# First head of a woven decoder layer: another order of its projection chunks

## The chip, the cores and the metric

The kernel runs on one core of one Trainium2 chip. The metric is the device time of one execution in microseconds (us). Engines are named as the profile names them: PE (TensorE matmuls), PEld (its weight loads), DVE (VectorE), ACT (ScalarE), POOL (GpSimd), SP (the queue that issues DMAs). A "column" below is one column that a matmul streams through the array; at the full granted clock of 2.4 GHz 2,400 columns take a microsecond.

## The reference, cut to what matters

A hybrid decoder layer on 2,064 tokens (16 meta tokens and 2,048 real ones) of width 1,024. One input projection feeds eight heads of stick-breaking attention and, beside them, a gated linear recurrence (RG-LRU); both are normalised, gated with a SiLU and go through one output projection.

```python
u = rmsnorm(h, pre_g)
q, k, v, g_att, x_lru, g_lru = jnp.split(u @ w_in, ...)       # six groups of 1,024 columns
att = rmsnorm(stick_breaking_attention(q, k, v), att_out_g) * jax.nn.silu(g_att)
lru = rmsnorm(rglru_branch(x_lru, ...), lru_out_g) * jax.nn.silu(g_lru)
y = jnp.concatenate([att, lru], axis=-1) @ w_out
return h + rmsnorm(y, post_g)
# attention, per query row: z = q.k * scale; w = exp(log_beta + suffix sum of log(1 - beta)); o = w @ v
# recurrence, per channel: conv of width 4, two gates (sigmoid of 64x64 blocks), h_t = a_t h_(t-1) + b_t
```

## The kernel before

**Tiling.** The projection, the scores and the attention outputs are made in two fp16 pieces, three matmuls for one product. A weight tile of 128 columns of `w_in` is loaded by `load_w`: DMA, a maximum over it (L144), a small matmul that spreads the maximum (L150), then the two pieces (L158 on ACT, L159 on DVE). There are buffers for three weights; a new one is loaded when the last chunk of an old one is done, in a fixed list: k, q, v, LRU gate, attention gate, LRU input of each head. A *chunk* is one weight against up to 512 tokens (8 x 3 matmuls at L174), into one of three PSUM tiles `mm`.

**Attention.** Each of the 16 query tiles of a head has one to three segments of keys. A segment is a chain over all engines: scores on PE (L301, into one of two PSUM tiles `z`), sigmoid on ACT (L305, frees `z`), a mask on POOL (L310), a product scan on DVE (L315), a cast on ACT (L325, L327), a subtraction on DVE (L332, L333), a DMA transpose (L338, `wT<-w`), and the output on PE (L352, `o<-wT,v`). After four query tiles ACT empties `o` (L385, L388).

**The recurrence.** Half a head's LRU input (three `xl` chunks, emptied at L458) makes one half of `Mix`: convolution on DVE (L474, L477), six gate steps (L485, L486, L496, L497, L498, L499), and then for both halves tanh, two exps, a square root on ACT (L507, L510, L514, L523, with ACT table loads wherever the function changes), products on DVE and POOL (L519, L527), a scan on DVE (L531), a square on ACT (L535) and a sum on POOL (L544). The first half of head 0's LRU is done before the attention starts, the second beside it.

**Order.** PE, ACT and DVE run in the order in which a planner emits the work (`weave`, a simulated clock with buffers as `Ring`s). At each step it takes, in this order: something urgent (gate steps, weight loads), the next attention output whose transposed weights are due, the next segment's scores if a `z` tile and a row buffer are free and its pace allows, and otherwise the next matmuls of the chunk that heads the list `fill`. `begin(h)` puts the chunks of head `h` on that list, `K` (k), `Q` (q), `VV` (v), `GL` (LRU gate), `GA` (attention gate) of head `h`, and `XL` (LRU input) of head `h+1`. Only the head of the list is looked at: if it may not start, no later chunk is taken. What holds a chunk back: its weight is not loaded; `GL` needs `"hs" in hd`, the finished recurrence of its head; `K` of a head needs all scores of the head before. `conv(c, m)`, the start of a half of the next head's `Mix`, needs the last `GL` chunk of the head before (`"used" in head[c - 1]`) and its three `XL` chunks.

Head 0's q, k and v are projected before the weave, so its list has only `GA`, `GL` and head 1's `XL`. The last head (7) is written out without the planner; behind it stands the output projection (L1380).

Of the kernel before, what the change touches and what calls it, by code (L numbers as in the profile page):

```python
# [70 lines left out]
def hybrid_layer(nc, tc, I, out):  # L71
# [107 lines left out]
    def unscale(w, f):  # L179
        t = sm.tile([P, 1], F32, name="us", bufs=6)  # L180
        dve.tensor_scalar(out=t, in0=w[2], scalar1=f, scalar2=None, op0=ALU.mult)
        return t
# [91 lines left out]
    def z_scale(wq, wk):  # L274

        t = sm.tile([P, 1], F32, name="zs", bufs=2)
        dve.tensor_scalar(out=t, in0=wq[2], scalar1=wk[2], scalar2=-SCALE / PSC ** 2, op0=ALU.mult, op1=ALU.mult)
        return t
# [538 lines left out]
    def k_then(h, j):  # L817
        def f(ps, t):
            if j == 0:
                kqv["kH"] = kp.tile([P, T], F16, name="kH")  # L820
                kqv["kL"] = kp.tile([P, T], F16, name="kL")
            c0, n = KV_CH[j]
            ev_pair(ps, t, n, kqv["kH"][:, c0:c0 + n], kqv["kL"][:, c0:c0 + n])
        return f
# [3 lines left out]
    def q_then(h, j):  # L828
        def f(ps, t):
            if j == 0:  # L830
                kqv["qH"] = kp.tile([P, S], F16, name="qH")
                kqv["qL"] = kp.tile([P, S], F16, name="qL")
            c0, n = Q_CH[j]
            ev_pair(ps, t, n, kqv["qH"][:, c0 - NM:c0 - NM + n], kqv["qL"][:, c0 - NM:c0 - NM + n])
            head[h]["q"] = t + 1.5 if j == NJ - 1 else None
        return f
# [105 lines left out]
    def ga_then(h, g):  # L942
        def f(ps, t):
            ev_silu(ps, t, head[h]["uga"], rsa, "sa", gate)

        def gate(gt, t):
            if (h, g) not in ots:
                waiting[h, g] = lambda t: gate(gt, t)
                return
            ot = ots.pop((h, g))  # L950
            dve.scalar_tensor_tensor(out=gt, in0=ot, scalar=prm(ATG, h), in1=gt, op0=ALU.mult, op1=ALU.mult)
            t = V(t, 512)
            rot.put(t)

            def store():
                sp.dma_start(out=aa_d[g][h], in_=gt)
                rsa.put(LD(t) - 2)
            plan.at(t, store)
        return f
# [219 lines left out]
    def begin(h):  # L1179

        c = h + 1
        hd = head.setdefault(h, {})
        hd.setdefault("v", [])
        head[c] = {"xs": [], "gates": 0, "v": []}
        hd["zdone"] = hd["odone"] = False

        def scale(to, hh, w):
            def f():
                head[hh][to] = unscale(loaded[w], 1.0)
            return f  # L1190

        def kq():
            hd["wk"] = loaded[f"k{h}"]

        def qs():
            hd["zs"] = z_scale(loaded[f"q{h}"], hd["wk"])

        def vs():
            hd["wv"] = loaded[f"v{h}"]
            hd["vsc"] = unscale(hd["wv"], 1.0 / (VSC * WS))  # L1200
        zs_done = lambda: h == 0 or head[h - 1]["zdone"]
        os_done = lambda: h == 0 or head[h - 1]["odone"]
        K = [Chunk(f"k{h}", *KV_CH[j], k_then(h, j), zs_done, kq if j == 0 else None, j == NJ - 1) for j in range(NJ)]
        Q = [Chunk(f"q{h}", *Q_CH[j], q_then(h, j), None, qs if j == 0 else None, j == NJ - 1) for j in range(NJ)]
        if h == H - 1:
            return K + Q
        VV = [Chunk(f"v{h}", *KV_CH[j], v_then(h, j), os_done, vs if j == 0 else None, j == NJ - 1) for j in range(NJ)]
        GA = [Chunk(f"ga{h}", NM + 512 * g, 512, ga_then(h, g), None, scale("uga", h, f"ga{h}") if g == 0 else None, g == 3)
              for g in range(4)]
        GL = [Chunk(f"gl{h}", NM + 512 * g, 512, gl_then(h, g), lambda: "hs" in hd,  # L1210
                    scale("ugl", h, f"gl{h}") if g == 0 else None, g == 3) for g in range(4)]
        XL = [Chunk(f"xl{c}", (m // 3) * HT + X_CH[m % 3][0], X_CH[m % 3][1], xl_then(c, m), None,
                    scale("uxl", c, f"xl{c}") if m == 0 else None, m == 5) for m in range(6)]
        if h == 0:
            return XL[:2] + GA[:1] + XL[2:4] + GA[1:2] + XL[4:] + GL[:2] + GA[2:] + GL[2:]
        return K + Q + VV + GL[:2] + GA[:1] + GL[2:] + GA[1:2] + XL[:3] + GA[2:] + XL[3:]

    def weave():
        fill, segs = [], []
        for h in range(H - 1):  # L1220
# [5 lines left out]
            segs += hs_  # L1226
        cost = [3.1 * x.L / 1000 + 1.2 for x in segs]
        fill += begin(0)
        nz = no = 0
        begun, due, pace = 0, 0.0, 0.0  # L1230
        while True:
# [37 lines left out]
            if not fill and begun < H - 1:  # L1269
                begun += 1  # L1270
                fill += begin(begun)
# [196 lines left out]
```

## Time and profile before

| | |
|---|---|
| median of 3 runs | 1951.55 us (1946.86 to 1952.28) |
| the profiled execution | 1950.06 us, its span 1948.3 us, mean granted clock 0.975 |
| PE busy | 1817.2 us, 93% of the span |
| DVE, ACT, POOL busy | 1280.1, 1038.4, 395.9 us |
| norms, k, q, v of head 0, first half of LRU 0 | 0 to 164 us |
| woven heads 0 to 6, with q and k of head 7 | 164 to 1443 us |
| head 7 and the output projection | 1443 to 1948 us |

A row of a timeline gives the start, the length and in brackets how long the engine was idle before it and what ended that. A row of stretches gives, for each engine, its busy time; then the granted clock as a share of 2.4 GHz. PE is busy for nearly all of the span, so what can be won is its idle time and the time that it ran at a lower clock.

### The profile page before, as it was taken

How to read it: one execution, taken by the hardware profiler on the slowest of the kernel's cores; microseconds unless marked ns; L12 is line 12 of the kernel's file. 1: busy time of each engine (PE TensorE's matmuls, PEld its weight loads, DVE VectorE, ACT ScalarE, POOL GpSimd, SP SyncE). 2: the span in 40 equal slices, each digit the busy share in tenths (PEclk: the TensorE clock that was granted, in tenths of full speed). 3: DMA queues.
4: the chain of work that ended last, by engine and by line, in shares of the span. 5: the costliest groups of instructions: out<-in, count | busy, mean ns of one | idle time of the engine just before them, and what ended most of it. 6: DMA issues, size and time to landing. Idle time of an engine off the chain costs nothing.

```text
span 1948.3 us, 30797 instructions
## 1 busy us (share of the span) xinstructions
PE 1817.2 (93%) x12048; PEld 1170.5 (60%) x12048; DVE 1280.1 (66%) x1761; ACT 1038.4 (53%) x1764; POOL 395.9 (20%) x460
## 2 busy tenths in 40 slices
PE   3879899699999899999998999999989899999998
PEld 2435565356546655665565566546645578888776
DVE  8546875787578857875895887579865761124554
ACT  6556745755556575556575555655665552132331
POOL 4421100510141132003120401041132010002222
PEclk9989999899999899999999999999999999999999
DMA  5922460364135616441553365146504693245554
GB/s 167 196 52 61 99 130 28 65 127 97 38 79 109 118 29 124 110 82 36 114 115 66 70 136 101 37 80 121 109 19 91 163 225 104 92 160 180 173 173 140
DMA packets 435809, 205.29 MB, mean 105 GB/s; under 512 B 370368, under 2 KB 404160, under 8 KB 435664
## 3 DMA queue, kind: packets, MB, share of 16 engines
q1 hardware_dynamic: 435664, 203.33, 44.3%
q8 instruction: 94, 1.54, 0.3%
q14 instruction: 51, 0.42, 0.1%
HBM read 78.23 MB, written 34.08 MB: 58 GB/s over the span
## 4 chain that ended last, share of the span: by engine, by line
PE 67%; DVE 5%; ACT 3%; DMA 3%; issue 1%; SPq 0%; POOL 0%; DVEq 0%; POOLq 0%; ACTq 0%
PE mm L174 34%; PE y L1380 18%; PE o L352 7%; PE z L301 6%; DMA wT<-w 2%; DVE row L315 1%; DVE lrow L531 1%; DVE w L333 1%; PE mm L496 1%; PE mm L497 0%; ACT lrow L499 0%; ACT row L498 0%; ACT ot L385 0%; DVE wm L144 0%; SPq L338 0%
## 5 line engine op out<-in xcount | busy, mean ns | idle before, releaser
L174 PE MATMUL mm<-uH,wH 128*128 128x512 f16 (+3 forms) x1808 | 624.6, 349 | 12.4 <-DVE qL L219 5.2
L174 PE MATMUL mm<-uL,wH 128*128 128x512 f16 (+3 forms) x1808 | 623.7, 348 | 1.5 <-DMA uL<-w 0.8
L174 PE MATMUL mm<-uH,wL 128*128 128x512 f16 (+3 forms) x1808 | 622.4, 348 | 2.7 <-DVE wL L159 2.7
L174 PEld LDWEIGHTS <-wH 128*128 128x128 f16 x3616 | 341.1, 99 | 310.0 <-issue 39.9
L315 DVE TENSOR_TENSOR_SCAN row<-row 128x656 f32<-128x656 f32 (+6 forms) x208 | 347.6, 1675 | 56.4 <-POOL row L310 47.2
L174 PEld LDWEIGHTS <-wL 128*128 128x128 f16 x1808 | 179.5, 99 | 164.3 <-issue 7.4
L352 PE MATMUL o<-wT,v 128*128 128x128 f16 x3392 | 229.5, 223 | 31.4 <-DMA wT<-w 30.9
L352 PEld LDWEIGHTS <-v 128*128 128x128 f16 x3392 | 211.4, 100 | 69.7 <-issue 35.7
L305 ACT ACTIVATE row<-z,zs 128x656 f32<-128x656 f32 (+6 forms) x208 | 170.7, 825 | 144.1 <-PE z L301 131.4
L333 DVE TENSOR_TENSOR w<-row,w 128x640 f16<-128x640 f32 (+5 forms) x208 | 175.7, 847 | 6.3 <-ACT w L327 5.9
L327 ACT CAST w<-row 128x640 f16<-128x640 f32 (+5 forms) x208 | 155.0, 747 | 41.9 <-DVE row L315 29.1
L301 PE MATMUL z<-kH,qH 128*128 128x328 f16 (+10 forms) x384 | 125.4, 327 | 18.7 <-ACT row L305 18.7
L1380 PE MATMUL y<-woH,aL 128*128 128x512 f32 x352 | 138.8, 394 | 1.2 <-DVE aL L1372 1.2
L1380 PE MATMUL y<-woH,aH 128*128 128x512 f32 x352 | 139.1, 395 | 0.0
L1380 PE MATMUL y<-woL,aH 128*128 128x512 f32 x352 | 138.5, 393 | 0.0
L301 PE MATMUL z<-kL,qH 128*128 128x328 f16 (+10 forms) x384 | 125.2, 326 | 0.0
L301 PE MATMUL z<-kH,qL 128*128 128x328 f16 (+10 forms) x384 | 125.0, 326 | 0.0
L310 POOL TENSOR_SCALAR_AFFINE_SELECT row<-row 128x128 f32<-128x128 f32 x128 | 67.0, 525 | 260.7 <-ACT row L305 243.6
L323 POOL MEMSET w<- 128x80 f16 x128 | 21.7, 169 | 469.1 <-DMA wT<-w 302.0
L486 DVE TENSOR_TENSOR cs<-lrow,cs 64x344 fp32r<-64x344 f32 x96 | 51.6, 538 | 95.9 <-ACT cs L485 88.6
L301 PEld LDWEIGHTS <-qH 128*128 128x128 f16 x768 | 73.2, 99 | 67.6 <-issue 22.3
L1372 DVE TENSOR_TENSOR aL<-araw,aH 128x1024 fp32r<-128x1024 f32 x32 | 39.2, 1224 | 110.4 <-ACT aH L1371 109.1
(225 smaller groups left out, 2544.4 us busy)
## 6 DMA issues: line engine op xcount, KB each, us to landing
wraw<-in_w_in SPq DMA_DIRECT2D x46, 512.0 KB, 3.8
row<-in_x SPq DMA_DIRECT2D x31, 512.0 KB, 4.4
aa_d<-sa SPq DMA_DIRECT2D x32, 256.0 KB, 2.0
al_d<-sl SPq DMA_DIRECT2D x32, 256.0 KB, 2.1
araw<-in_w_out SPq DMA_DIRECT2D x16, 512.0 KB, 4.5
araw<-al_d SPq DMA_DIRECT2D x16, 512.0 KB, 4.1
yl_d<-ys SPq DMA_DIRECT2D x32, 256.0 KB, 2.1
row<-yl_d SPq DMA_DIRECT2D x16, 512.0 KB, 3.2
```

The costliest lines, as they stand in the source:

```text
L174: pe.matmul(out=ps[:, :n], lhsT=a[:, kt, :], rhs=b[:, kt, c0:c0 + n], start=(k == 0), stop=(k == 3 * KT - 1))
L301: pe.matmul(out=z[:, a, :n], lhsT=l[:, qs], rhs=r[:, c], start=(x == 0), stop=(x == 2))
L305: act.activation(out=self.om[:, :L].rearrange("p (a c) -> p a c", a=self.parts), in_=self.z[:, :self.parts, :self.n], func=AF.Sigmoid, sca ...
L310: pool.affine_select(out=d, in_=d, pattern=[[-1, P]], compare_op=ALU.is_gt, fill=1.0, base=0, channel_multiplier=1)
L315: dve.tensor_tensor_scan(out=om, data0=om, data1=om, initial=self.pred.om[:, 0:1] if self.si else WS, op0=ALU.mult, op1=ALU.bypass)
L323: pool.memset(w[:, 3 * NM:P], 0.0)
L327: act.copy(out=w[:, r0:r0 + nb * P], in_=om[:, self.m0:self.L])
L333: dve.tensor_tensor(out=w[:, r0 + nb * P:r0 + 2 * nb * P], in0=om[:, self.m0:self.L], in1=w[:, r0:r0 + nb * P], op=ALU.subtract)
L352: pe.matmul(out=o[:, c], lhsT=l, rhs=r, start=(self.si == 0 and x == 0), stop=(self.last and x == len(prods) - 1))
L486: dve.tensor_tensor(out=cs[oth, :n], in0=xc[own, a:a + n], in1=cs[own, :n], op=ALU.subtract)
L1372: dve.tensor_tensor(out=aL, in0=raw, in1=aH, op=ALU.subtract)
L1380: pe.matmul(out=ps, lhsT=a[:, c, :], rhs=b[:, cs], start=(k == 0), stop=(k == 3 * KT - 1))
```

## The change

One expression in `begin`: the list of head 0's fill chunks.

```diff
         if h == 0:
-            return XL[:2] + GA[:1] + XL[2:4] + GA[1:2] + XL[4:] + GL[:2] + GA[2:] + GL[2:]
+            return GA[:2] + XL[:3] + GL + XL[3:] + GA[2:]
         return K + Q + VV + GL[:2] + GA[:1] + GL[2:] + GA[1:2] + XL[:3] + GA[2:] + XL[3:]
```

The chunks are the same; no instruction is added or taken away. Before, all six `xl` chunks of head 1 came ahead of the four `gl` chunks of head 0. Now the second half of the `xl` chunks stands behind `gl`, and the first two `ga` chunks lead. Because the planner goes on from the state that it is in, the order changes in all later woven heads too.

ACT in head 0, from the second exp of its recurrence (L514) on; `row<-z` are sigmoids of scores, by segment length:

```order
L514 ACTIVATE row<-row,nsp_m_76 128x1032
L305 ACT_TABLE_LOAD
L305 ACTIVATE row<-z,zs 128x640
L325 CAST w<-row 128x2x16
L327 CAST w<-row 128x512
L305 ACTIVATE row<-z,zs 128x656
L523 ACT_TABLE_LOAD
```

```order
L514 ACTIVATE row<-row,nsp_m_76 128x1032
L305 ACT_TABLE_LOAD
L305 ACTIVATE row<-z,zs 128x640
L325 CAST w<-row 128x2x16
L327 CAST w<-row 128x512
L305 ACTIVATE row<-z,zs 128x528
L523 ACT_TABLE_LOAD
```

The 640 in the first piece belongs to query tile 9 (segments of 640 and 656), in the second to tile 8 (640 and 528): the recurrence now stands one query tile earlier.

PE in head 1, at the scores of its query tiles 5 (2 x 392 columns) and 6 (2 x 456):

```order
L301 LDWEIGHTS qL
L301 MATMUL z<-kH,qL 128x392
L301 LDWEIGHTS qH
L301 MATMUL z<-kH,qH 128x456
L301 LDWEIGHTS qH
L301 MATMUL z<-kL,qH 128x456
```

```order
L301 LDWEIGHTS qL
L301 MATMUL z<-kH,qL 128x392
L174 LDWEIGHTS wH
L174 MATMUL mm<-uH,wH 128x512
L174 LDWEIGHTS wH
L174 MATMUL mm<-uL,wH 128x512
```

Before, one tile's scores were followed by the next tile's; now matmuls of a `gl` chunk of head 1 stand between.

PE near the end of head 4, behind the scores of the first segment (2 x 384 columns) of query tile 15:

```order
L301 LDWEIGHTS qL
L301 MATMUL z<-kH,qL 128x384
L352 LDWEIGHTS v
L352 MATMUL o<-wT,v 128x128
L352 LDWEIGHTS v
L352 MATMUL o<-wT,v 128x128
```

```order
L301 LDWEIGHTS qL
L301 MATMUL z<-kH,qL 128x384
L174 LDWEIGHTS wH
L174 MATMUL mm<-uH,wH 128x344
L174 LDWEIGHTS wH
L174 MATMUL mm<-uL,wH 128x344
```

Before, only outputs and scores were left there (no chunk stood between); now chunks of head 5's `xl` do.

## Rows read from the trace of the kernel before

**Rows 1.** The page: busy time by engine; the chain that ended last.
```profile
PE 1817.2 (93%) x12048; PEld 1170.5 (60%) x12048; DVE 1280.1 (66%) x1761; ACT 1038.4 (53%) x1764; POOL 395.9 (20%) x460
...
PE 67%; DVE 5%; ACT 3%; DMA 3%; issue 1%; SPq 0%; POOL 0%; DVEq 0%; POOLq 0%; ACTq 0%
```

**Rows 2.** Stretches: length; busy PE, PEld, DVE, ACT, POOL; clock, DMA, GB/s.
```profile
214.00:227.00 13.00, 7.86 (x61) 5.11 (x60) 11.21 (x10) 9.61 (x15) 4.64 (x7) 0.74 0.24 56
281.00:352.00 71.00, 69.40 (x425) 38.62 (x423) 45.44 (x81) 36.63 (x79) 9.81 (x14) 1.00 0.20 51
352.00:402.00 50.00, 34.01 (x211) 18.67 (x210) 40.58 (x40) 37.55 (x55) 23.56 (x18) 0.80 0.32 69
402.00:650.00 248.00, 247.32 (x1803) 149.95 (x1802) 180.88 (x255) 147.89 (x253) 45.22 (x62) 1.00 0.44 89
650.00:672.00 22.00, 13.31 (x120) 10.81 (x118) 19.08 (x23) 10.48 (x15) 2.13 (x4) 0.77 0.47 105
672.00:895.00 223.00, 221.90 (x1610) 133.06 (x1609) 156.70 (x224) 131.98 (x230) 39.74 (x57) 1.00 0.41 85
895.00:1065.00 170.00, 163.44 (x1227) 101.67 (x1226) 131.45 (x177) 102.78 (x182) 40.84 (x50) 0.99 0.43 92
1065.00:1270.00 205.00, 203.46 (x1450) 120.82 (x1449) 148.57 (x213) 121.63 (x210) 40.57 (x55) 1.00 0.40 82
1270.00:1427.00 157.00, 150.45 (x1140) 94.03 (x1138) 126.91 (x166) 95.69 (x168) 36.47 (x46) 0.99 0.48 98
1443.00:1456.00 13.00, 8.41 (x60) 6.00 (x58) 11.70 (x15) 4.78 (x8) 5.12 (x3) 0.87 0.01 3
```

**Rows 3.** PE's timeline in head 1, then at head 4's start: start, us, row, idle.
```profile
366.35 0.54 PE L301 MATMUL z<-kH,qH 128*128 128x456 f16 x1 [5.05 <-ACT row L305]
...
388.05 0.38 PE L301 MATMUL z<-kH,qH 128*128 128x264 f16 x1 [2.81 <-ACT row L305]
...
929.72 0.30 PE L301 MATMUL z<-kH,qH 128*128 128x328 f16 x1 [1.67 <-ACT row L305]
```

**Rows 4.** PE's timeline at the ends of heads 2 and 4.
```profile
657.65 2.40 PE L352 MATMUL o<-wT,v 128*128 128x128 f16 x21 [4.17 <-DMA wT<-w]
...
1028.69 2.40 PE L352 MATMUL o<-wT,v 128*128 128x128 f16 x24 [3.78 <-DMA wT<-w]
```

**Rows 5.** PE's timeline in head 0: its stall, and a row ahead of it.
```profile
199.97 0.38 PE L174 MATMUL mm<-uH,wH 128*128 128x512 f16 x1
...
221.22 0.26 PE L150 MATMUL mm<-dg,onesb 128*128 128x128 bf16 x1 [3.19 <-ACT lrow L458]
222.61 0.59 PE L174 MATMUL mm<-uH,wH 128*128 128x512 f16 x1 [1.13 <-ACT lrow L458]
```

**Rows 6.** ACT's timeline in head 0.
```profile
196.44 0.62 ACT L327 CAST w<-row 128x512 f16<-128x512 f32 x1 [1.63 <-DVE row L315]
...
200.24 0.61 ACT L327 CAST w<-row 128x512 f16<-128x512 f32 x1
200.87 1.28 ACT L305 ACT_TABLE_LOAD   x1
202.17 0.70 ACT L305 ACTIVATE row<-z,zs 128x528 f32<-128x528 f32 x1
202.76 0.68 ACT L905 ACTIVATE sa<-mm,us 128x512 f32<-128x512 f32 x1
...
205.37 1.16 ACT L514 ACTIVATE row<-row,nsp_m 128x1032 f32<-128x1032 f32 x1
```

**Rows 7.** The DMA transposes of line 338, 164 to 285 us: issue, and time to landing.
```profile
L338 SPq DMA_TRANSPOSE wT<-w x26: 1185/1439/2656, 169.2 to 272.9; - x26
...
DMA to landing us min/median/max: 2.3/3.6/5.4
```

**Rows 8.** DVE's, then PE's timeline where head 7 begins.
```profile
1440.53 4.45 DVE L531 TENSOR_TENSOR_SCAN lrow<-lrow 128x1032 f32<-128x1032 f32 x1 [0.90 <-POOL lrow L527]
...
1448.58 0.22 PE L150 MATMUL mm<-dg,onesb 128*128 128x128 bf16 x1 [4.59 <-DVE dg L147]
```

## The prediction

> **What bounds the kernel now.** The page first: PE is busy for 93% of the span, and the chain that ended last lies on PE for 67% [rows 1]. No instruction comes or goes, so the time can change only where PE waits or runs below its full clock. I therefore read the stretches next and price each as idle time plus busy time x (1 - granted clock). From 164 to 214 and from 227 to 281 us PE has no idle time. The rest of the woven part [rows 2]:
>
> - 214 to 227 us, head 0: 5.14 idle + 7.86 x 0.26 = 7.2 us.
> - 281 to 352, k, q, v of head 1: 1.6 us.
> - 352 to 402, start of head 1: 15.99 + 34.01 x 0.20 = 22.8 us.
> - 402 to 650, rest of head 1 and most of head 2: 0.7 us.
> - 650 to 672, end of head 2: 8.69 + 13.31 x 0.23 = 11.8 us.
> - 672 to 895, head 3: 1.1 us. 1065 to 1270, head 5: 1.5 us.
> - 895 to 1065, head 4: 6.56 + 1.6 = 8.2 us. 1270 to 1427, head 6: 6.55 + 1.5 = 8.1 us.
> - 1443 to 1456, entry of head 7: 4.59 + 8.41 x 0.13 = 5.7 us.
>
> Together 68.7 us, all that the change can reach; behind 1456 us the order of head 7 and of the output projection stays nearly as it was.
>
> Then the waits in these stretches. In head 1 scores wait for the sigmoid that frees their `z` tile, 5.05 and 2.81 us [rows 3]; at the ends of heads 2 and 4 outputs wait for transposed weights, 4.17 and 3.78 us [rows 4]. Both are the chain of a segment, and PE feels it only where it has nothing else to do. The order of before says where that is. Counted from it, the stretches with two or more segments of scores, over 7,500 columns and no chunk or gate step between are five: 7,984 columns in head 0, 11,664 in head 1, 19,680 at the end of head 2, 14,896 each at the ends of heads 4 and 6. These are the five places of the large losses. Heads 3 and 5 have none and lose 1.1 and 1.5 us. I call such a stretch bare.
>
> **The change part by part.** The order of after has one bare stretch over 7,500 columns in heads 0 to 6: 16,224 columns in head 0, between the third `xl` chunk and the first `gl` chunk. So the working is: what is that stretch worth, and what do the removed ones give back.
>
> *Head 0.* `gl` may not start before the recurrence is done, and the chunks that used to cover that time (`xl` 4 to 6) now stand behind `gl`. PE comes to the bare stretch as early as before, since the columns ahead of it are the same in number and were free of waits. Inside it the last score needs the sigmoid of tile 8's second segment (528 columns). In before that sigmoid started at 202.17 and ended at 202.9 [rows 6]. In front of it ACT now has the same instructions plus the second exp (1.16) with two table loads (2 x 1.28) and one more gate sigmoid (0.68), 4.4 us; in before it had idled 1.63 us there [rows 6], which may or may not go. So it ends between 205.6 and 207.3. PE had as many columns behind it as that score has ahead of it at 200.4, by the row at 199.97 [rows 5] and 1,088 columns more. The wait is 5.2 to 6.9 us; I take 6. Next, the output of tile 7's second segment stands only 4,608 columns (1.9 us) behind that score. Its cast ends as that sigmoid starts, near 206; a subtraction, the transpose's issue (1.4) and landing (3.6) [rows 7] put the output past 211, and PE is there near 209: I take 3 us. Two scores in a row shortly after cost perhaps 1 us. Ten us idle; the end of head 2 paid 3.1 us of clock for 8.7 idle, so 3 more: **13 us**. The nearest rows bound it: head 4, with 14,896 bare columns, at 8.2, and head 1, where both halves of the recurrence end beside the scores, at 22.8. The one half here is nearer to the middle, so I keep 13. The old stall of 7.2 us (PE waited 3.19 and 1.13 us for the last `xl` chunks to be emptied [rows 5]) goes, since only three of them are left there.
>
> A page of the Trainium skill speaks against this price: ScalarE: Activation LUTs, "What ACT_TABLE_LOAD costs", gives a switch of function a drain of 1.38 us beside the load's 1.28. The trace doesn't show that drain: a cast ends at 200.85, the load begins at 200.87, and the sigmoid follows at 202.17 [rows 6]. By the page the two added loads would make the first wait 2.8 us longer, and the sum 2.8 us less.
>
> DVE, too, gets work in head 0: the first convolution of head 1's recurrence, since its condition (the last `gl` chunk) now holds earlier. In before DVE did it between 281 and 352, where it is busy for only 45 of 71 us [rows 2]. It is not on PE's path by itself; if that cover is gone, it is a few us inside the bounds above.
>
> *Head 1.* Because its convolution starts earlier and its `xl` chunks end earlier against its q and v, all twelve gate steps stand before v, not among it and the first scores, and the end of the recurrence falls into the 50,000 columns (21 us) of v. `gl` is then free when the scores start: the order has chunks of `gl` between all of them up to tile 6. The two rows of 5.05 and 2.81 us have no place any more. I take 2 us in place of 22.8 + 0.7, with the 0.7 of a well-fed stretch as the lower end and half of the old price as the upper one. The k, q, v stretch stays at 1.6.
>
> *Heads 2 to 6.* Their order in after is the same five times over, and it is none of before's orders; so one unknown is paid five times. Its ends are fed: the last scores and outputs stand among `xl` and k chunks. Nearest are heads 3 and 5, which are fed in the same way, at 1.1 and 1.5. The far end is head 4, at 8.2. I take 2.0 each, a little above the near end, because two scores follow each other at the start of each head, which cost 1.67 us where before had that [rows 3]: 10 us, in place of 11.8 + 1.1 + 8.2 + 1.5 + 8.1 = 30.7.
>
> *Entry of head 7.* PE waited 4.59 us for the small matmul of a weight load, whose input stood on DVE behind the recurrence's scan of 4.45 us [rows 8]. In after that input stands ahead of the scan. But the gate steps end 13,000 columns (5.4 us) later there, so something of it may stay: 2 us in place of 5.7, from 0 to 5.7.
>
> **How the terms add.** 13 + 1.6 + 2 + 10 + 2 = 28.6 us in place of 68.7: 40 us less. Against the profiled execution's own 1950.06 that is 1910; the median of the three runs lies 1.5 above it, so I say **1911**.
>
> **The rivals.**
>
> *The bare stretch of head 0 is dear.* Its waits come in several short pieces; if PE falls to the lower clock and stays there, as in 352 to 402 (0.80 over 50 us), it costs as much as that did, 22.8: 10 us more, **1921**. By the page TensorE: Matmul & The Clock Gate of the Trainium skill (Part 1), PE is granted its full clock only after sustained work, so that such pieces would run at half rate; 16,224 columns would then cost another 6.8 us. The trace agrees as far as it goes: 0.74 to 0.80 in the stretches with stalls, 1.00 in the others [rows 2]. For it: ACT is the engine waited for. Against it: one half of a recurrence, not two.
>
> *The five equal heads behave like heads 4 and 6.* If their order has a wait that I can't see in it, 8.2 us each: 41 in place of 10, 31 us more, **1942**. For it: no head of before has exactly that order. Against it: nothing bare is left in it, and every large loss of before was bare.
>
> *Slower.* The same five-fold wait, but as large as the end of head 2, 11.8 us each, with the bare stretch at 22.8: 22.8 + 1.6 + 2 + 59 + 2 = 87, 19 us above 68.7: **1970**. The place would be each head's outputs, if the transposes came late by some 4 us twice per head. It decides from about 10 us per head on (68.7 - 18.6 spread over five). Against it: the transposes' landing of 3.6 us is hidden wherever a chunk stands between.
>
> That the change does nothing is excluded: the order differs from head 0 to head 6.
>
> **How the numbers follow.** Forecast 0.68; dear stretch 0.16; heads like 4 and 6 0.08; slower 0.05; 0.03 for something near no change. What a measurement of this kernel can tell from no change is about 0.3%, 6 us. Faster holds the first three, 0.92; same 0.03; slower 0.05. For the range: the lower bounds together (8.2 + 1.6 + 0.7 + 5.5 + 0 = 16) give 1899, and a few us below for what my prices of waits miss: 1894. Upwards it takes in the dear stretch and most of the way to the third case: 1937.
>
> **What would show it.** In the changed profile: PE idle with "ACT row L305" and "DMA wT<-w" as releasers between about 194 and 215 us, 8 to 12 us of it, and none near 216 to 222; the start of head 1 (near 350 us) without idle pieces over 1 us; the ends of heads 2, 4 and 6 without waits for `wT`; five heads that lose the same to within 1 us, under 3 us each. If they are equal but lose over 5 us each, the second rival holds. If head 0's stall is under 5 us, the ACT sum above is wrong.

## The result, and the profile after

The changed kernel takes 1918.4 us (median of four runs, 1912.9 to 1922.9) where before takes 1951.15, measured beside it: a ratio of 0.9835, 95% interval 0.9803 to 0.9866. It is 32.7 us faster; 40 were forecast, and the time lies 7 us above the forecast and inside the range. The profiled execution took 1922.94, the slowest of the four, so the two profiles differ by 27.1.

The page of the changed kernel, busy time by engine (before: [rows 1]):

```profile
PE 1809.9 (94%) x12048; PEld 1160.5 (60%) x12048; DVE 1280.8 (67%) x1761; ACT 1038.5 (54%) x1764; POOL 406.8 (21%) x460
```

Its stretches, with the columns of [rows 2]. The heads have moved: head 1's first score is at 340 us, head 2's at 518, head 7's at 1399. The rows of 12 us lie around the first outputs of heads 2 to 6.

```profile
190.00:226.00 36.00, 28.49 (x255) 19.07 (x253) 27.49 (x29) 31.46 (x47) 11.64 (x14) 1.00 0.52 99
...
281.00:340.00 59.00, 58.35 (x374) 33.09 (x372) 33.21 (x62) 38.07 (x67) 7.32 (x8) 1.00 0.10 34
340.00:376.00 36.00, 31.64 (x155) 15.14 (x154) 31.50 (x39) 23.16 (x41) 21.52 (x15) 0.95 0.34 72
376.00:460.00 84.00, 83.70 (x689) 54.94 (x688) 73.02 (x92) 53.98 (x94) 15.89 (x25) 1.00 0.53 108
460.00:490.00 30.00, 27.06 (x241) 17.83 (x239) 19.41 (x28) 12.92 (x24) 1.92 (x5) 1.00 0.58 119
490.00:518.00 28.00, 27.45 (x174) 15.25 (x171) 14.82 (x25) 20.78 (x30) 4.17 (x3) 1.00 0.09 29
...
540.00:552.00 12.00, 11.31 (x76) 6.08 (x75) 9.11 (x15) 6.95 (x17) 4.09 (x7) 1.00 0.61 129
...
719.00:731.00 12.00, 10.26 (x71) 5.55 (x70) 8.69 (x13) 6.21 (x15) 4.11 (x7) 1.00 0.66 126
898.00:910.00 12.00, 9.92 (x56) 4.75 (x55) 7.60 (x12) 5.28 (x11) 3.94 (x7) 0.86 0.72 117
1079.00:1091.00 12.00, 9.74 (x54) 4.65 (x52) 7.66 (x12) 5.22 (x11) 3.87 (x6) 0.86 0.67 116
1260.00:1272.00 12.00, 10.01 (x56) 4.82 (x55) 7.81 (x12) 5.47 (x11) 4.75 (x7) 0.86 0.60 121
...
1416.00:1437.00 21.00, 20.59 (x120) 10.75 (x120) 18.39 (x29) 9.43 (x17) 13.80 (x7) 1.00 0.04 9
1437.00:1460.00 23.00, 19.10 (x114) 10.02 (x113) 16.00 (x31) 14.14 (x31) 5.61 (x13) 0.93 0.37 74
```

Priced as the prediction prices them (idle time plus busy time x (1 - clock)), term by term in us:

| term | before | forecast | measured |
|---|---|---|---|
| head 0 (190 to 226) | 7.2 | 13 | 7.5 |
| k, q, v of head 1 (281 to 340) | 1.6 | 1.6 | 0.7 |
| head 1 (340 to 518) | 23.5 | 2 | 5.9 + 0.3 + 2.9 + 0.6 = 9.7 |
| heads 2 to 6 (518 to 1416) | 30.7 | 10 | 15.6 |
| entry of head 7 (1416 to 1460) | 5.7 | 2 | 0.4 + 5.2 = 5.6 |
| sum | 68.7 | 28.6 | 39.1 |

Of the 15.6, the five rows of 12 us hold 0.7 + 1.7 + 3.5 + 3.6 + 3.4 = 12.9; the other 838 us of these heads hold 2.7 (their idle time, at a clock of 1.00). So the sum fell by 29.6. Two misses upwards (head 1, and those five stretches) and one downwards (head 0) make the difference to the forecast, besides the entry of head 7, which gained nothing. The two profiles differ by 27.1 us and not by 29.6; the other 2.5 are in no stretch priced here, and the clock of a stretch is given to two places only, which in the longest ones is worth almost 1 us.

### The profile page after: what moved, and what is told of

It is laid out like the page before. It is cut to its first block, busy times and chain, and to the rows that moved or that the text cites. A ratio compares the mean times of both kernels' runs of the same rounds, so it can differ in the third digit from the quotient of the medians.

```text
span 1921.0 us, 30849 instructions
## 1 busy us (share of the span) xinstructions
PE 1809.9 (94%) x12048; PEld 1160.5 (60%) x12048; DVE 1280.8 (67%) x1761; ACT 1038.5 (54%) x1764; POOL 406.8 (21%) x460
## 4 chain that ended last, share of the span: by engine, by line
PE 72%; DVE 10%; DMA 7%; ACT 6%; issue 4%; POOL 1%; SPq 1%; DVEq 0%; POOLq 0%; ACTq 0%
PE mm L174 38%; PE y L1380 18%; PE o L352 8%; PE z L301 6%; DMA wT<-w 4%; DVE row L315 2%; DVE lrow L531 1%; DVE w L333 1%; DMA wraw<-in_w_in 1%; ACT row L305 1%; PE mm L496 1%; ACT lrow L499 1%; DVE wL L159 1%; PE mm L497 1%; ACT w L327 0%
## 5 line engine op out<-in xcount | busy, mean ns | idle before, releaser
L315 DVE TENSOR_TENSOR_SCAN row<-row 128x656 f32<-128x656 f32 (+6 forms) x208 | 342.2, 1647 | 53.8 <-POOL row L310 30.5
L352 PE MATMUL o<-wT,v 128*128 128x128 f16 x3392 | 224.8, 220 | 29.5 <-DMA wT<-w 29.3
L305 ACT ACTIVATE row<-z,zs 128x656 f32<-128x656 f32 (+6 forms) x208 | 170.6, 825 | 149.4 <-PE z L301 135.1
L352 PEld LDWEIGHTS <-v 128*128 128x128 f16 x3392 | 207.4, 99 | 69.1 <-issue 34.3
L327 ACT CAST w<-row 128x640 f16<-128x640 f32 (+5 forms) x208 | 155.3, 747 | 19.5 <-DVE row L315 11.7
L310 POOL TENSOR_SCALAR_AFFINE_SELECT row<-row 128x128 f32<-128x128 f32 x128 | 86.5, 676 | 232.8 <-ACT row L305 224.4
L301 PE MATMUL z<-kH,qH 128*128 128x328 f16 (+10 forms) x384 | 123.9, 323 | 12.5 <-ACT row L305 12.5
L301 PEld LDWEIGHTS <-qH 128*128 128x128 f16 x768 | 72.7, 98 | 62.2 <-issue 16.2
L1414 POOL TENSOR_TENSOR row<-row 128x512 f32<-128x512 f32 x32 | 46.6, 1455 | 295.5 <-ACT row L1413 279.3
```

Of the source, the lines that this page charges most:

```text
L301: pe.matmul(out=z[:, a, :n], lhsT=l[:, qs], rhs=r[:, c], start=(x == 0), stop=(x == 2))
L305: act.activation(out=self.om[:, :L].rearrange("p (a c) -> p a c", a=self.parts), in_=self.z[:, :self.parts, :self.n], func=AF.Sigmoid, sca ...
L310: pool.affine_select(out=d, in_=d, pattern=[[-1, P]], compare_op=ALU.is_gt, fill=1.0, base=0, channel_multiplier=1)
L315: dve.tensor_tensor_scan(out=om, data0=om, data1=om, initial=self.pred.om[:, 0:1] if self.si else WS, op0=ALU.mult, op1=ALU.bypass)
L327: act.copy(out=w[:, r0:r0 + nb * P], in_=om[:, self.m0:self.L])
L352: pe.matmul(out=o[:, c], lhsT=l, rhs=r, start=(self.si == 0 and x == 0), stop=(self.last and x == len(prods) - 1))
```

## The experiments

The losses below are priced in the same way. Some expectations count head 1 over more than its start, and so name 27 us for before and 11 for the changed kernel, where the stretch from 340 to 402 us has 24.0 and 6.1.

### The changed kernel again

No edit; a second profile.

> The changed kernel once more, for a second profile. Theory A (the shortfall lies in the transfers): in the first profile of the changed kernel heads 2 to 6 run one and the same PE order, yet behind their first outputs they lost 0.8, 1.9, 3.9, 4.1 and 3.8 us, where a weight load of 512 KB is issued 0.7 and 2.0 us ahead of two transposes of attention weights; the second transpose then held its queue for 2.0 to 3.6 us in place of 1.2. If that is contention, the same five places lose again, but by other amounts (each 0.5 to 4.5 us), and the run differs from the first profile mostly there. Theory B (the order itself is short of work at that place): the five places lose the same amounts as before, in the same sequence. Time by both 1912 to 1923.

Measured: 1917.7 us (four runs, 1916.0 to 1918.5). The five stretches lost 0.9, 1.8, 3.8, 1.8 and 1.9 us; two of them:

```profile
898.00:910.00 12.00, 9.59 (x51) 4.90 (x50) 7.26 (x12) 4.98 (x12) 4.09 (x7) 0.86 0.78 122
1079.00:1091.00 12.00, 10.20 (x71) 5.52 (x70) 8.13 (x14) 6.37 (x15) 4.12 (x7) 1.00 0.63 122
```

The places are the same. Head 5 lost 1.8 us here and 3.6 in the first profile, but 1.4 of that difference is the clock (1.00 here, 0.86 there). PE's idle time alone is 0.9, 1.8, 2.4, 1.8 and 1.9 us here and was 0.7, 1.7, 2.1, 2.3 and 2.0: nearly the same wait in the same head, which is what theory B expects, and what contention that comes back in the same way would show too. So this run doesn't decide between the two. What stands there in head 4 of the first profile, the transposes of line 338 by themselves:

```profile
L338 SPq DMA_TRANSPOSE wT<-w x2: 1222/2394/3565, 899.7 to 901.1; - x2
...
DMA to landing us min/median/max: 5.6/5.7/5.8
```

The weight load of 512 KB was issued at 899.07. The transposes behind it land after 5.6 to 5.8 us, where 3.6 is the median of before [rows 7], and the second one held the queue for 3.57 us. The load is late as well: it lands after 5.7 us, where the median of all 46 such loads is 3.9.

### The load held back

```diff
+        dve.memset(raw[:, 0, 0:1], 0.0) if late else None
         sp.dma_start(out=raw, in_=I["w_in"][col])
+        if late: yield
...
-            next(parts)
+            next(parts) if name[:2] not in ('xl',) else [plan.at(plan.free["pe"] + d, lambda: next(parts)) for d in (4.0, 8.5)]
```

> The changed kernel, with the load of the LRU input's weight (one per head, started when v is done) held back by about 4 us behind a one-element write on DVE, and its maximum by 8.5 us; PE, ACT and the rest of DVE keep their order. Theory A (the load delays the transposes next to it): the losses at the first outputs of heads 1 to 6 (1.8, 0.8, 1.9, 3.9, 4.1, 3.8, together 16 us) fall below 1 us each, the transposes there hold their queue for 1.2 us, and the time falls by 8 to 15 us, to 1903 to 1910. Theory B (those outputs are late for want of work on PE, whatever the load does): the losses stay and the time stays at 1918 within 4 us. A third possibility: the load meets other transposes 4 us later that are also waited for, and the time stays although the waits move.

Measured: 1959.4 us (five runs), 41 us slower than the changed kernel; a miss. The one-element write stands in DVE's order, and DVE reaches it late: in heads 2 to 4 the load is issued 11 to 13 us after its old place, 0.7 us ahead of the third query tile's transpose. The small matmul of the weight (L150) then waits for its input, 7.5 us in head 4, PE's only wait over 0.2 us between 925 and 940 us. The outputs of heads 2 to 6 waited for no transpose any more, which is the half of theory A that this run could show.

### The load held back less

The same edit with 2.5 and 4.5 in place of 4.0 and 8.5.

> The load held back again, but less: the one-element write that releases it stands on DVE right behind the subtraction of the next segment (640 columns), and the load's maximum behind the scan of 912, so that the small matmul of the weight should find its input ready (about 553 us in head 2 against the 555 us at which PE comes to it); in the run with the longer hold PE waited for that input 6 to 8 us in each of heads 1 to 6, and this hid what the hold gave. PE and ACT keep the order of the changed kernel. Theory A (the load lengthens the two transposes that stand behind it): no loss over 1 us at the first outputs of heads 2 to 6 (2 to 4 us each before), transposes of 1.2 us there, 8 to 12 us less than the changed kernel: 1906 to 1910. Theory B (the load only has to be out of the way somewhere, and any place costs the same): the loss moves to the next outputs, 1914 to 1922.

Measured: 1936.6 us (five runs), again a miss in the time and for the same reason. PE's only wait over 0.2 us between 905 and 925 us:

```profile
922.29 0.23 PE L150 MATMUL mm<-dg,onesb 128*128 128x128 bf16 x1 [4.18 <-DVE dg L147]
```

My estimate of when DVE would come to the write (about 4 us after the old place) was wrong: in head 4 the load was issued at 916.5, and the old place, 0.7 us ahead of the third query tile's transpose, is at 906.4 in this run. The first outputs again waited for nothing. Two runs thus show the waits at the outputs gone with the load, but neither shows what that is worth, since a dearer wait took their place.

### The load issued by ACT

```diff
-        sp.dma_start(out=raw, in_=I["w_in"][col])
+        (act if 34 <= col < 40 else sp).dma_start(out=raw, in_=I["w_in"][col])
```

> The changed kernel, with the same six weight loads issued at the same point from ACT's DMA queue and not from SP's, so that nothing stands ahead of the transposes in their queue. If the load delays them by standing ahead of them in the queue: transposes of 1.2 us right behind it, and a time as with the load held back, 1903 to 1910. If it delays them by taking the DMA engines' time: the transposes land as late as before, the losses at the first outputs of heads 2 to 6 stay at 2 to 4 us, and the time stays at 1918 within 4 us.

Measured: 1911.6 us (four runs, 1909.1 to 1913.2), between the two theories. In head 4, the transposes at the same place:

```profile
L338 SPq DMA_TRANSPOSE wT<-w x2: 1259/2018/2778, 898.8 to 900.3; - x2
...
DMA to landing us min/median/max: 4.9/5.1/5.4
```

With nothing ahead of them in their own queue they still land 1.3 to 1.8 us late. So the place in the queue isn't the reason, or not the only one: the load takes the time of the DMA engines. The run changed two things, the queue and the moment of issue (ACT starts the load 1.4 us ahead of the first of the two transposes, SP did 0.7), so which of them brought the 6 to 7 us that it gained isn't shown. The Trainium skill says the same (DMA: Bandwidth & Descriptors, "Issuing engines are not separate DMA queues"): transfers from whatever engine run on the same 16 DMA engines and interleave. The trace agrees, with 5.1 us against 5.7 from SP's queue and 3.6 to 3.7 where the load is out of the way (next).

### The load issued earlier

```diff
+    def ahead(name):
+        early[name] = load_w(ctile["xl"] + int(name[-1]), split=True)
+        next(early[name])
...
-            parts = load_w(ctile[name[:-1]] + int(name[-1]))
+            parts = early.pop(name, None) or load_w(ctile[name[:-1]] + int(name[-1]))
...
+            ahead(order[cursor[0] - 1]) if self.name[0] == "v" and self.name != "v1" and self.c0 == KV_CH[4][0] else None
```

In `load_w` the load moves to the front, with `if split: yield` behind it.

> The changed kernel; only the LRU input's weight load of heads 2 to 6 is issued earlier, where the last v chunk starts and not where it ends: three transposes further up in SP's queue. PE, ACT and DVE keep their order, the load's maximum included. Theory A (the load, when it is issued right ahead of the two transposes of the head's first outputs, lengthens them and delays its own maximum on DVE): losses at those outputs below 1 us each (2 to 4 in the changed kernel), transposes there of 1.2 us, no new wait since the load's maximum has its input early: 6 to 11 us less than the changed kernel, 1907 to 1912. Theory B (any transposes beside the load are late): the loss moves to the outputs before, whose transposes now stand behind the load, and the time stays at 1918 within 4 us.

Measured: 1908.0 us (five runs, 1906.4 to 1912.2; ratio to before 0.9795, interval 0.9777 to 0.9813), 10 us faster than the changed kernel by the medians and 8 by the ratios to before (0.9795 and 0.9835), each measured beside its own runs of before. That is as theory A has it, and the best version of this study. The five stretches (moved with the heads):

```profile
540.00:552.00 12.00, 12.00 (x80) 6.45 (x79) 10.53 (x15) 6.89 (x17) 2.28 (x7) 1.00 0.55 105
717.00:729.00 12.00, 11.51 (x77) 6.17 (x76) 8.98 (x15) 5.61 (x13) 3.29 (x7) 1.00 0.81 123
895.00:907.00 12.00, 12.00 (x80) 6.38 (x79) 9.99 (x16) 6.85 (x16) 3.80 (x7) 1.00 0.74 130
1072.00:1084.00 12.00, 12.00 (x80) 6.43 (x79) 9.54 (x15) 6.21 (x14) 3.06 (x7) 1.00 0.69 123
1249.00:1261.00 12.00, 11.77 (x79) 6.23 (x77) 8.84 (x15) 5.60 (x12) 2.95 (x7) 1.00 0.67 108
```

They lose 0.7 us together, in place of 12.9. The transposes of head 4:

```profile
L338 SPq DMA_TRANSPOSE wT<-w x2: 1249/1436/1623, 897.6 to 899.1; - x2
...
DMA to landing us min/median/max: 3.6/3.7/3.7
```

PE, ACT and DVE run the same order as in the changed kernel; five loads are issued 7 to 8 us ahead of the first of those transposes and not 0.7 (1.7 in head 5), which is five transposes further up in SP's queue. Nine of the ten transposes land after 2.9 to 3.7 us, where they took 4.1 to 5.8; the tenth, in head 3, still takes 5.2, and PE waits 0.5 us for it. This settles heads 2 to 6: their order costs almost nothing, and what they lost was the load beside the transposes.

### GL undivided, the rest of the list as before

```diff
-            return XL[:2] + GA[:1] + XL[2:4] + GA[1:2] + XL[4:] + GL[:2] + GA[2:] + GL[2:]
+            return XL[:2] + GA[:1] + XL[2:4] + GA[1:2] + XL[4:] + GL + GA[2:]
```

> The kernel before with one thing changed in head 0's list: the two GA chunks that stood between the halves of GL stand behind it (XL[:2], GA[:1], XL[2:4], GA[1:2], XL[4:], GL, GA[2:]). Its order in heads 2 to 6 is that of the changed kernel; head 0 keeps the two short bare stretches of before (7,984 and 6,960 columns), and head 1 starts with 8,208 bare columns in place of 11,664. Theory by bare stretches, priced from the two profiles: head 0 as before, head 1 some 8 us less than before, heads 2 to 6 13 us less: 1951 - 21 = 1930, between 1924 and 1936. Rival (what head 0 itself does with its front part makes the gain): no gain, 1945 to 1952. Rival (all of the gain is the order of heads 2 to 6): 1918 within 4 us.

Measured: 1933.8 us (five runs, ratio 0.9916, interval 0.9902 to 0.9929): 16.8 us of the 33, with two GA chunks moved behind GL and nothing else. The sum is as expected, but one part of it isn't. Head 1's start, 340 to 402 us, in before and here:

```profile
340.00:402.00 62.00, 45.80 (x278) 24.96 (x276) 49.90 (x53) 45.30 (x71) 28.24 (x24) 0.83 0.37 76
```

```profile
340.00:402.00 62.00, 49.47 (x273) 25.82 (x272) 47.47 (x51) 44.03 (x67) 24.89 (x22) 0.86 0.36 78
402.00:480.00 78.00, 75.80 (x616) 48.81 (x613) 63.30 (x77) 44.27 (x74) 6.56 (x17) 1.00 0.53 110
```

Before loses 16.2 + 45.8 x 0.17 = 24.0, this kernel 12.5 + 6.9 = 19.5 and another 2.2 in the stretch behind it, which before has at full work: some 2 us less, where 8 were expected for 8,208 bare columns in place of 11,664.

### Only GA in front

```diff
-            return XL[:2] + GA[:1] + XL[2:4] + GA[1:2] + XL[4:] + GL[:2] + GA[2:] + GL[2:]
+            return GA[:2] + XL + GL + GA[2:]
```

> Head 0's list with the two GA chunks in front and nothing else of the change (GA[:2], XL, GL, GA[2:]). Its order has 6,704 bare columns in head 0, none in head 1, and 14,896 each at the ends of heads 2, 4 and 6, as before has at heads 4 and 6. Theory by bare stretches: head 1 loses 5 to 11 us in place of 27, head 2 9.5 in place of 13.5, heads 3 to 6 lose what they lost before, head 0 3 to 9 in place of 9: 1951 - 16 - 4 - 3 = 1928, between 1920 and 1934. Rival (the gain needs XL split around GL): 1945 to 1952.

Measured: 1944.9 us (five runs, ratio 0.9965, interval 0.9953 to 0.9978): 5.5 us, where 23 were expected; a miss. Head 1's start:

```profile
340.00:402.00 62.00, 49.08 (x284) 25.52 (x283) 47.96 (x61) 44.02 (x72) 26.25 (x24) 0.92 0.38 80
```

It loses 12.9 + 3.9 = 16.9 us, and its longest bare stretch there has 5,776 columns (354.7 to 362.1 us), half of before's. PE's timeline: the first of these waits lies inside that stretch; the other two come with matmuls of `gl` chunks before and behind them, and all are nearly as long as in before.

```profile
360.97 0.30 PE L301 MATMUL z<-kH,qH 128*128 128x328 f16 x1 [4.50 <-ACT row L305]
...
371.96 0.54 PE L301 MATMUL z<-kH,qH 128*128 128x456 f16 x1 [3.43 <-ACT row L305]
...
387.89 0.98 PE L352 MATMUL o<-wT,v 128*128 128x128 f16 x13 [3.57 <-DMA wT<-w]
```

So "bare" alone isn't what prices head 1. The rival, that the gain needs XL split around GL, came out at its edge in the time (1945 to 1952). As a whole it doesn't hold, for GL undivided gained 16.8 us with all of XL ahead of GL; for head 1 it does: only the two lists with GL between the halves of XL bring its loss below 16 us. What the lists do share is where the end of head 1's recurrence lies. First score of head 1 and first scan of its recurrence (L531), against the loss from 340 to 402 us:

| list | first score | first scan | longest bare stretch, columns | loss |
|---|---|---|---|---|
| before | 329.0 | 374.8 | 11,664 | 24.0 |
| GL undivided | 329.8 | 371.4 | 8,208 | 19.5 |
| GA in front | 333.7 | 369.6 | 5,776 | 16.9 |
| changed | 340.3 | 355.6 | under 5,000 | 6.1 |
| XL in front (next) | 339.1 | 340.7 | under 5,000 | 1.4 |

### XL in front

```diff
-            return GA[:2] + XL[:3] + GL + XL[3:] + GA[2:]
+            return XL[:3] + GL + XL[3:] + GA
```

> Head 0's list with XL[:3] at its front and both GA chunks behind (XL[:3], GL, XL[3:], GA). Its order has one bare stretch, 23,312 columns in head 0 (16,224 in the changed kernel), and head 1 already runs the order of heads 2 to 5, so that the end of its recurrence does not meet its first scores. Theory (bare columns cost in proportion, the rest as in the changed kernel's profiles): head 0 15 us in place of 10, head 1 4 us in place of 11, so 1918 - 2 = 1916, between 1911 and 1921. Rival (a longer bare stretch keeps PE at the lower clock, as at head 1's start before the change): head 0 some 23 us, 1922 to 1928.

Measured: 1919.5 us (five runs, 1917.8 to 1921.7), level with the changed kernel, as expected and for the expected reason: head 1's start loses 1.4 us in place of 6.1, and head 0 is dearer.

```profile
340.00:402.00 62.00, 60.57 (x397) 33.77 (x396) 52.54 (x77) 36.24 (x71) 23.17 (x29) 1.00 0.49 104
...
165.00:190.00 25.00, 19.65 (x152) 13.78 (x151) 18.06 (x28) 21.15 (x47) 7.65 (x11) 0.97 0.28 54
190.00:230.00 40.00, 35.60 (x278) 23.06 (x276) 34.08 (x33) 31.69 (x46) 8.70 (x16) 0.89 0.50 98
```

From 165 to 230 us it loses 5.4 + 0.6 + 4.4 + 3.9 = 14.3, where the changed kernel loses 7.6.

With the early load added to this list:

> The list of xl_first (XL[:3], GL, XL[3:], GA) with the early load, in heads 1 to 6. Head 1 lost 3.3 us there in place of 11, head 0 some 8 us more than in the changed kernel. If the gains add up: 1919 less 6 to 12, 1907 to 1913, no better than the early load alone. If the early load takes nothing here either: 1916 to 1922.

Measured: 1909.2 us (four runs, 1907.4 to 1910.0). The 10 us of the early load are there again, and the list itself is still worth nothing beside the changed one.

### Head 1's recurrence without table loads

```diff
-            act.activation(..., func=AF.Exp, ...)
+            act.activation(..., func=AF.Tanh if self.c == 1 else AF.Exp, ...)
...
-            act.activation(..., func=AF.Sqrt)
+            act.activation(..., func=AF.Tanh if self.c == 1 else AF.Sqrt)
```

> The kernel before; in head 1 alone the exps and square roots of the recurrence are replaced by tanh (this part of the result is left out), so that ACT loads no other table: six loads of 1.28 us go, nothing else changes on any engine. Theory C (head 1 loses 27 us because the end of its recurrence runs on ACT and DVE beside its first scores): the chain there gets 7.7 us shorter, and the loss of head 1 falls by 5 to 12 us, to 15 to 22; time 1939 to 1946. Theory D (it loses them because no chunk stands between its scores, by the 11,664 bare columns): the order is the same, the loss falls by 3 us at most; time 1947 to 1952.

Tanh needs no load behind a sigmoid: in before a sigmoid starts at 193.07 us and a tanh follows at 193.66. So a load doesn't stand at every change of function, and this edit takes all six away.

Measured: 1947.2 us (ten runs, ratio 0.9990, interval 0.9980 to 0.9999). Head 1's start loses 14.3 + 6.7 = 21.0 us, 3 less:

```profile
340.00:402.00 62.00, 47.69 (x284) 26.09 (x284) 49.45 (x52) 37.87 (x65) 29.51 (x24) 0.86 0.40 78
```

Theory C had 5 to 12. ACT was given back 7.4 us (45.30 busy before, 37.87 here), and 3 of them reached PE. By themselves the table loads are worth 3 of the 24 us.

### The end of head 1's recurrence made thin

```diff
-            self.c, ..., self.cs = c, ..., {}
+            self.c, ..., self.cs, self.w = c, ..., {}, 32 if c == 1 else HT
...
-            act.activation(out=s[:, :HT], in_=self.rs[m][:, :HT], func=AF.Tanh, ...)
+            act.activation(out=s[:, :self.w], in_=self.rs[m][:, :self.w], func=AF.Tanh, ...)
```

and so in every step from the tanh to the sum. In the kernel before:

> The kernel before, with the end of head 1's recurrence made thin: each of its tanh, exp, square root, product, scan, square and sum works on 32 columns in place of 1,032 (the rest of head 1's recurrence is left out). The order on PE, ACT, DVE and SP is that of before, bare columns and table loads included; POOL changes the place of a few rows. Theory C (head 1's 27 us of loss are the work of the recurrence's end on ACT, DVE and POOL beside its first scores): the loss falls below 10 us, the time to 1932 to 1937. Theory D (the loss is the segment's own chain, felt because 11,664 columns there have no chunk between them): the loss falls by 6 us at most, 1943 to 1950. Between the two, the shares follow from the loss that stays.

Measured: 1940.7 us (four runs, ratio 0.9947, interval 0.9933 to 0.9962). In the changed kernel:

> The changed kernel with the same thin end of head 1's recurrence (the rest of it left out; order as in the changed kernel). In its profiles head 1 lost 11 us; the waits of 2.7 us for a z tile stood behind the squares on ACT, which stood behind the scans on DVE. Theory C: these go, head 1 loses 6 to 8 us (what stays are about 2 us at its first output and 4 us beside a weight load in the middle of the head), 1913 to 1916. Theory D (that wait is the chain of the segment itself): 1916 to 1920.

Measured: 1911.5 us (four runs, 1907.8 to 1917.6), below both ranges. Their spread overlaps that of the changed kernel, so the trace tells more here than the time. Head 1's start, in the one and in the other:

```profile
340.00:402.00 62.00, 53.75 (x357) 30.67 (x356) 45.01 (x65) 43.44 (x84) 16.97 (x28) 0.89 0.55 104
```

```profile
340.00:402.00 62.00, 62.00 (x419) 35.06 (x418) 46.91 (x77) 36.60 (x75) 12.79 (x29) 1.00 0.54 113
```

Before falls from 24.0 to 8.3 + 5.9 = 14.2: 9.8 of its loss are the length of the recurrence's work beside the scores. Neither theory was right alone. The 14.2 that stay are not all the segments' own chain: the thin run keeps the table loads, and two of them, at 360.53 and 365.74 us, stand on ACT right ahead of the sigmoids for which PE waits 2.68 and 2.87 us. No run has both the work and the loads taken away, so how much of the 14.2 is the segments' own chain stays open. In the changed kernel the loss goes from 6.1 to nothing: what was left there was all the recurrence's end.

## Why the prediction was right, and where it was not

**The direction, the places and the size.** The gain came from head 1 (13.8 us) and from heads 2 to 6 (15.1), as forecast, and head 0 gave nothing. That it was 33 and not 40 us comes from the terms below. The errors partly cancel (head 0 with k, q, v was put 6 us too dear, the other three terms 17 too cheap); that the total came nearer than its terms is luck.

**Heads 2 to 6: 10 forecast, 15.6 measured.** The order was judged rightly, even too dearly: with the load out of the way these heads have 0.6, 1.1, 0.6, 0.6 and 0.6 us of idle time, 3.4 together, and the two scores at the start of a head cost 0.2 us, not the 1.67 that I had counted. The step that failed is "one unknown is paid five times", priced from the heads of before that are fed. I looked for what stands between scores on PE and not for what else the DMA engines carry there. In the changed order a weight load is issued 0.7 us ahead of the transpose of a head's third query tile, for which PE waits, and 2.0 us ahead of the fourth's (1.7 and 3.0 in head 5). I counted transposes at their landing of 3.6 us [rows 7]; these took up to 5.8. That the five equal heads would lose the same to within 1 us was wrong too: their first outputs lost 0.7 to 3.6 us (0.7 to 2.3 of it idle time, the rest clock), in an order that is the same.

**Head 1: 2 forecast, 9.7 measured.** The failed step is "the end of the recurrence falls into the 50,000 columns (21 us) of v". The gate steps did stand before v, but the end was longer than v: from its first tanh (330.85 us) to the end of its second square (364.06) it took 33 us, and PE was through with v at 351.0. ACT's, DVE's, POOL's and PE's timelines of the changed kernel:

```profile
363.00 1.06 ACT L535 ACTIVATE row<-lrow 128x1032 f32<-128x1032 f32 x1 [1.36 <-DVE us L181]
...
366.51 0.70 ACT L305 ACTIVATE row<-z,zs 128x528 f32<-128x528 f32 x1
```

```profile
355.58 4.47 DVE L531 TENSOR_TENSOR_SCAN lrow<-lrow 128x1032 f32<-128x1032 f32 x1
...
360.61 2.35 DVE L531 TENSOR_TENSOR_SCAN lrow<-lrow 128x1032 f32<-128x1032 f32 x1
```

```profile
354.99 2.90 POOL L527 TENSOR_TENSOR lrow<-lrow,row 128x1032 f32<-128x1032 f32 x1
```

```profile
352.68 0.38 PE L352 MATMUL o<-wT,v 128*128 128x128 f16 x4 [1.66 <-DMA wT<-w]
...
367.25 0.49 PE L301 MATMUL z<-kH,qH 128*128 128x392 f16 x1 [2.70 <-ACT row L305]
```

The second square (L535) waits on ACT until DVE is through with the second scan, a score's sigmoid (L305) stands behind it on ACT, and PE waits for the `z` tile until that sigmoid ends at 367.2. The first scan took 2.1 us more than the second; POOL's product was running when it started (last section). The run with the thin end takes PE's two waits away. The other 2.9 us lie in the middle of the head (460 to 490), where a transpose was issued 1.0 us behind a weight load and held the queue for 3.13 us; no run took that apart.

The rule by which I chose the places, that PE feels the chain of a segment only where nothing else stands between, was half right. It named the ends of heads 2, 4 and 6 correctly: from 530 us to head 7, before is idle for 24.4 us and the list with only GA in front, which keeps those stretches, for 22.6; the one with GL undivided, which has none, for 10.9. It failed for head 1, where "GA in front" loses 16.9 us with no bare stretch over 5,776 columns.

**Head 0: 13 forecast, 7.5 measured.** The waits came where they were worked out, between 194 and 215 us, but cut up otherwise. PE's and ACT's timelines:

```profile
196.82 1.22 PE L352 MATMUL o<-wT,v 128*128 128x128 f16 x19 [1.65 <-DMA wT<-w]
...
204.86 0.30 PE L301 MATMUL z<-kH,qH 128*128 128x320 f16 x1 [2.85 <-ACT row L305]
...
210.88 0.89 PE L352 MATMUL o<-wT,v 128*128 128x128 f16 x13 [1.59 <-DMA wT<-w]
```

```profile
196.12 1.16 ACT L510 ACTIVATE lrow<-row,nsp_m 128x1032 f32<-128x1032 f32 x1
197.29 1.28 ACT L305 ACT_TABLE_LOAD   x1
198.58 0.70 ACT L305 ACTIVATE row<-z,zs 128x528 f32<-128x528 f32 x1
...
205.34 0.70 ACT L305 ACTIVATE row<-z,zs 128x528 f32<-128x528 f32 x1
```

The sigmoid that I put between 205.6 and 207.3 ends at 206.0, and PE had waited 5.4 us by then, in four pieces, the first and the last of them above (5.2 to 6.9 worked out, 6 taken). All four stand ahead of the last score, which itself no longer waited. The output behind it waited 1.6 (3 taken), and the 3 us for the clock did not come: 1.00 through the stretch. The step that failed most is that price of the clock, taken from the end of head 2. The prediction's "0.74 to 0.80 in the stretches with stalls" had left out the stalls at other values: 0.87 at 1443 us, 0.99 over heads 4 and 6 [rows 2]. The drain of 1.38 us at a change of function, which the Trainium skill gives (ScalarE: Activation LUTs, "What ACT_TABLE_LOAD costs"), isn't seen here either: the exp ends at 197.28, the load starts at 197.29, and the sigmoid follows it at 198.58.

**Entry of head 7: 2 forecast, 5.6 measured, 5.7 before.** The wait of 4.59 us [rows 8] went, down to 0.4 in 1416 to 1437. The step that failed took it for the last one there: another stood behind it. PE's timeline, then ACT's:

```profile
1440.90 0.33 PE L301 MATMUL z<-kH,qH 128*128 128x400 f16 x1 [3.12 <-ACT row L305]
```

```profile
1431.22 1.15 ACT L158 ACTIVATE wH<-wraw,wm 128x1024 f16<-128x1024 f32 x1 [4.09 <-DVE wm L155]
...
1439.17 1.28 ACT L305 ACT_TABLE_LOAD   x1
1440.47 0.76 ACT L305 ACTIVATE row<-z,zs 128x144 f32<-128x144 f32 x2
```

ACT waits 4.1 us for the weight's scale from DVE, then has the casts of the norm and of v ahead of the first sigmoids, so those end at 1441. In before PE came to this point 4.6 us later than its order alone would have brought it, and the sigmoids were done. This is read from the traces; no run was made for it. They agree on it: the list with GL undivided has 0.4 and then 3.1 us as well, the one with only GA in front 4.57 and then no wait at the score.

**The range and the rivals.** The measured time lies nearest the first rival's 1921, and that is chance: the dear stretch of head 0 did not come. Of the second rival, which had the five equal heads at 8.2 each, the form came true (one wait, paid five times), at 3.1 each. The cause stood in the third, the slower case, which put it at "each head's outputs, if the transposes came late by some 4 us twice per head": they came late by 0.5 to 2.2 us, PE waited for one of the two, and a kernel slower than before did not come of it.

## What to carry to other kernels

Before pricing a new order from the fed heads of the old one, look at what is issued on the DMA queue within a few us ahead of each transfer that somebody waits for: here five loads, issued some 6 us earlier, were worth 8 to 10 us with the order on PE, ACT and DVE unchanged. A stretch without filler work is a reason for a wait, but not the only one: work of other engines that stands in order ahead of the waited instruction makes PE wait even where matmuls lie between. And when a stall is struck out, follow the waiting engine on to its next wait before booking the gain.

## What the runs showed of the hardware

- With a 512 KB load issued 0.7 us ahead of the first (1.7 in head 5), two transposes land after 4.1 to 5.8 us; with the same load 7 to 8 us ahead, after 2.9 to 3.7 but for one of 5.2. The delay differs by head and comes back in the second profile: 4.1 to 4.4 and 4.3 to 4.6 in head 2, 5.6 to 5.8 and 5.9 to 6.1 in head 4. With the load in ACT's queue, 1.4 us ahead, they take 4.9 to 5.4 in head 4.
- The granted clock answered alike pieces differently. Around 190 to 230 us the changed kernel waits 1.65, 0.48, 0.46 and 2.85 us at a clock of 1.00; with the early load, the same order waits 1.67, 0.47, 0.45 and 2.86 us and has 0.91:

```profile
190.00:230.00 40.00, 34.55 (x280) 22.39 (x278) 31.38 (x31) 34.39 (x51) 13.75 (x15) 0.91 0.48 93
```

Why is left open.
- The scan of 1,032 columns (L531) took 4.47 or 2.35 us in two places of one kernel, 5 us apart. In the traces of before and of the changed kernel every such scan over 2.5 us has a product or sum of POOL running when it starts, and is longer than 2.3 us by about what POOL still had to do: 4.47 with 2.3 us left of L527 (above), 2.83 at 527.57 with 0.7 left of L867. Where the scan starts first, it takes 2.3 us and POOL is the one that is late: in before the scan at 912.46 took 2.30, and L527 at 912.93 took 4.00, where at 1078.17, ahead of its scan, it took 2.37. These instructions act as if only one of the two engines could run them at a time; that is read from the traces, and no run tested it.
